# A softmax with its rows cut into ten tiles of thirteen and twelve rows instead of eleven of twelve and eight

## The chip, the cores and the metric

The kernel runs on one core of a Trainium2 chip. The metric is device time in microseconds, the median of several runs; lower is better. Besides, one execution of the kernel was recorded by the hardware profiler. Its times count from the first instruction of the program ("span").

A core has several engines that run their own instruction streams beside each other. Here three compute: VectorE (DVE) takes maxima and divides, ScalarE (ACT) takes exponentials, GpSimd (POOL) does next to nothing but issue transfers. SyncE (SP) only issues transfers. Transfers between the large memory (HBM) and the on-chip memory run on 16 DMA engines, which all queues share. Each stream is executed in order, and an instruction that waits holds up all behind it on its engine.

## The reference

The input is x of 32 x 512 rows with 1024 float32 each, and a temperature of 0.5. Each row is scaled and goes through a softmax:

```python
scaled = x / temperature
shifted = scaled - np.max(scaled, axis=-1, keepdims=True)
exp_x = np.exp(shifted)
return (exp_x / np.sum(exp_x, axis=-1, keepdims=True)).astype(np.float32)
```

So 67.1 MB are read and 67.1 MB written, and every element is looked at three times on the chip: for the maximum, for the exponential (with the sum of the row taken along), and for the division.

## The kernel before, in words

The 16384 rows are 128 for each of 128 partitions. They are cut into eleven tiles. A tile of k rows holds k rows of 4 KB in each partition, and takes a block of 128 x k neighbouring rows, so that each partition's share is one contiguous piece of k x 4 KB in HBM. The list `PASSES` (line 10) names the tiles, and how each is split into groups for the computation: `[4, 4, 4]`, nine times `[6, 6]`, and `[4, 4]`. Each number is the rows of a group; a tile's rows are their sum: 12 for ten tiles, 8 for the last. In this text tiles count from 0, so that tile 10 is the last.

A tile is loaded into one of four buffers by one transfer (line 60, issued by SP), computed in place, and stored by one transfer (line 108). With 12 rows of 4 KB, four buffers hold 48 rows, 192 KB in each partition. The pool of buffers goes round: tile i uses the buffer of tile i - 4, so its load waits until the store of tile i - 4 has landed.

For each group the kernel does three things:

- `maximum`: one instruction on DVE for the maxima of all rows of the group (line 69), and a small one that turns them into the bias -max/temperature (line 72).
- `exponential`: one instruction on ACT for each row (line 78), exp(x/temperature + bias), which also gives the row's sum.
- `divide`: the reciprocals of the sums (line 90, DVE), then the division, as one DVE instruction over the whole group (line 93) for the tiles in `WHOLE`, or one for each row (line 96) for the others.

`store` does something only with the last group of a tile: it issues the tile's transfer and then the load that waits for it. The stores of the tiles below `BY_POOL` are issued by POOL, the others by ACT. Ahead of the first store POOL reads one element of tile 2, and so waits until tile 2 has been loaded.

The order is written out by hand, and no scheduler changes it. In the loop over the groups the maximum and the exponential of group g stand ahead of the division and the store of group g - 1. So DVE has always a maximum to do while ACT takes exponentials. For the first group of a tile from `ALONE` on the order is turned round: the group before is divided and its tile stored first. In ACT's stream a store that ACT issues stands at the same place: behind the exponentials of the next tile's first group, or, from `ALONE` on, ahead of them.

Of the kernel before, what the change touches and what calls it, by code (L numbers as in the profile page):

```python
# [1 line left out]

# [4 lines left out]

PASSES = [[4, 4, 4]] + [[6, 6]] * 9 + [[4, 4]]  # L10
BUFS = 4

WHOLE = (2, 3, 4, 6, 8)


BY_POOL = 6

ALONE = 9


@with_exitstack
def kernel(
    ctx: ExitStack,
    tc: tile.TileContext,
    x: bass.AP,
    temperature: bass.AP,
    out: bass.AP,
):
    nc = tc.nc
    f32 = mybir.dt.float32  # L30
    scale = 1.0 / float(temperature)
    extreme = mybir.AluOpType.max if scale > 0 else mybir.AluOpType.min

    P = 128
    xf = x.flatten_outer_dims()
    of = out.flatten_outer_dims()
    n, d = xf.shape
    rows = [sum(ks) for ks in PASSES]
    assert sum(rows) * P == n

    data = ctx.enter_context(tc.tile_pool(name="data", bufs=BUFS))
    stats = ctx.enter_context(tc.tile_pool(name="stats", bufs=4))


    groups = []
    for i, ks in enumerate(PASSES):
        for j, k in enumerate(ks):
            groups.append((i, sum(ks[:j]), k))

    def dram(t, i):  # L50
        block = t[P * sum(rows[:i]) : P * sum(rows[: i + 1]), :]
        return block.rearrange("(p k) d -> p k d", p=P, k=rows[i])

    tiles, small = [], []

    def load():
        i = len(tiles)
        if i < len(PASSES):
            xt = data.tile([P, rows[i], d], f32, name="xt")
            nc.sync.dma_start(out=xt, in_=dram(xf, i))  # L60
            tiles.append(xt)

    def maximum(g):
        i, a, k = groups[g]
        top, bias, sums, recip = (
            stats.tile([P, k], f32, name=name) for name in ("top", "bias", "sums", "recip")
        )
        small.append((bias, sums, recip))
        nc.vector.tensor_reduce(  # L69
            out=top, in_=tiles[i][:, a : a + k, :], axis=mybir.AxisListType.X, op=extreme  # L70
        )
        nc.vector.tensor_scalar_mul(bias, in0=top, scalar1=-scale)  # L72

    def exponential(g):
        i, a, k = groups[g]
        bias, sums, _ = small[g]
        for b in range(k):
            nc.scalar.activation(  # L78
                tiles[i][:, a + b, :],
                tiles[i][:, a + b, :],  # L80
                mybir.ActivationFunctionType.Exp,
                bias=bias[:, b : b + 1],
                scale=scale,
                accum_out=sums[:, b : b + 1],
            )

    def divide(g):
        i, a, k = groups[g]
        _, sums, recip = small[g]
        nc.vector.reciprocal(recip, sums)  # L90
        if i in WHOLE:
            xt = tiles[i][:, a : a + k, :]
            nc.vector.tensor_mul(xt, xt, recip.unsqueeze(2).to_broadcast([P, k, d]))  # L93
            return
        for b in range(k):
            nc.vector.tensor_scalar_mul(  # L96
                tiles[i][:, a + b, :], in0=tiles[i][:, a + b, :], scalar1=recip[:, b : b + 1]
            )

    def store(g):  # L100
        i, a, k = groups[g]
        if a + k == rows[i]:
            if i == 0:


                nc.gpsimd.tensor_copy(stats.tile([P, 1], f32, name="seen"), tiles[2][:, 0, 0:1])  # L106
            queue = nc.gpsimd if i < BY_POOL else nc.scalar
            queue.dma_start(out=dram(of, i), in_=tiles[i])  # L108
            load()

    with tc.manual_schedule():
        for _ in range(BUFS):
            load()
        for g in range(len(groups) + 1):

            alone = g < len(groups) and groups[g][0] >= ALONE and groups[g][1] == 0
            if g > 0 and alone:
                divide(g - 1)  # L120
                store(g - 1)
            if g < len(groups):
                maximum(g)
                exponential(g)
            if g > 0 and not alone:
                divide(g - 1)
                store(g - 1)


# [1 line left out]
_INS = ['x', 'temperature']  # L131
_OUTS = [((32, 512, 1024), 'float32')]

_NUMBERS = {'temperature': 0.5}


# [26 lines left out]
```

## Time and profile before

| what | value |
|---|---|
| median of 3 runs | 317.25 us (317.19 to 320.41) |
| span of the profiled execution | 315.8 us |
| DVE busy | 256.9 us (81%) |
| ACT busy | 148.3 us (47%) |
| POOL busy | 3.7 us (1%) |
| mean rate of the DMA engines | 425 GB/s |
| maximum of 6 rows / of 4 rows (line 69) | 6547 ns / 4413 ns |
| exponential of one row (line 78) | 1135 ns |
| division of 6 rows at once (line 93) | 6558 ns |
| division of one row (line 96) | 749 ns |
| load of 12 rows, issue to landing, median | 36.4 us |
| store of 12 rows, issue to landing, median | 35.9 us by POOL, 31.9 us by ACT |

How to read it: the durations are those of single instructions as the profiler recorded them; neighbours on one engine overlap a little (row-wise divisions start 0.68 us apart, row-wise exponentials 1.13 us). "Issue to landing" holds all the time in which a transfer shares the DMA engines with others. A maximum of 6 rows costs 1.07 us for each row and some 0.1 us besides.

Between the span and the time of a run lies what is ahead of the program's first and behind its last recorded instruction: the median of the runs is 1.5 us above the span of the profiled execution.

### The profile page before, as it was taken

What the parts mean: (1) busy time and instruction counts of PE and PEld (TensorE: products, weight loads), DVE (VectorE), ACT (ScalarE), POOL (GpSimd) and SP (SyncE); (2) the same over time, 40 slices, a digit from 0 to 9 for tenths busy, and PEclk for the clock granted to TensorE, in tenths of its full rate; (3) what the DMA queues carried; (4) which work ended last, traced back from release to release, by engine and by line L of the source; (5) the groups of instructions that cost most, each with busy time, mean ns of one, the idle gap of its engine ahead of it and who ended that gap; (6) DMA issues with size and microseconds to landing.
All of it is one profiled execution on the core that took longest, in us unless ns stands there. A gap on an engine that the chain in (4) does not pass through costs nothing.

```text
span 315.8 us, 525 instructions
## 1 busy us (share of the span) xinstructions
DVE 256.9 (81%) x147; ACT 148.3 (47%) x257; POOL 3.7 (1%) x11
## 2 busy tenths in 40 slices
DVE  0069999999999899979976994999199999969710
ACT  0029636775461807344471744074416802953700
POOL 0000001000000000000000000000000000000000
DMA  8999999999999999999999999999999999999996
GB/s 305 473 417 423 461 411 399 399 468 430 400 479 417 417 461 411 430 467 405 442 448 399 455 442 405 467 424 417 461 417 430 455 401 463 411 452 411 455 411 270
DMA packets 3171, 134.24 MB, mean 425 GB/s; under 512 B 352, under 2 KB 352, under 8 KB 352
## 3 DMA queue, kind: packets, MB, share of 16 engines
q1 hardware_dynamic: 1584, 67.11, 49.7%
q0 software_dynamic: 864, 37.75, 27.6%
q10 hardware_dynamic: 720, 29.36, 21.5%
q14 instruction: 3, 0.02, 0.0%
HBM read 67.11 MB, written 67.11 MB: 425 GB/s over the span
## 4 chain that ended last, share of the span: by engine, by line
DMA 47%; DVE 28%; ACT 11%; issue 9%; DVEq 0%; SPq 0%; POOLq 0%
DMA xt<-in_x_dram 25%; DMA out_dram<-xt 22%; DVE top L69 16%; ACT xt L78 11%; DVE xt L96 8%; DVE xt L93 2%; DVE bias L72 0%; DVE recip L90 0%; DVEq L158 0%; SPq L60 0%; POOLq L108 0%
## 5 line engine op out<-in xcount | busy, mean ns | idle before, releaser
L78 ACT ACTIVATE xt<-xt,bias 128x1024 f32<-128x1024 f32 x128 | 145.2, 1135 | 131.7 <-DVE recip L90 70.6
L69 DVE TENSOR_REDUCE top<-xt 128x6 f32<-128x6144 f32 (+1 forms) x23 | 139.9, 6083 | 37.8 <-DMA xt<-in_x_dram 37.8
L93 DVE TENSOR_TENSOR xt<-xt,recip 128x6144 f32<-128x6144 f32 x10 | 65.6, 6558 | 0.4
L96 DVE TENSOR_SCALAR xt<-xt,recip 128x1024 f32<-128x1024 f32 x68 | 46.2, 749 | 0.5
L78 ACT ACTIVATION_READ_ACCUMULATOR xt<-xt,bias 128x1 f32 x128 | 23.9, 187 | 0.0
L78 ACT ACT_TABLE_LOAD x1 | 1.3, 1283 | 18.3 <-DMA xt<-in_x_dram 18.3
L90 DVE RECIPROCAL recip<-sums 128x6 f32<-128x6 f32 (+1 forms) x23 | 4.2, 182 | 5.0 <-ACT xt L78 5.0
L108 POOL DMA_DIRECT2D out_dram<-xt x6 | 3.3, 554 | 129.6 <-ACT xt L78 82.7
L72 DVE TENSOR_SCALAR bias<-top 128x6 f32<-128x6 f32 (+1 forms) x23 | 3.9, 171 | 0.8
L106 POOL COPY seen<-xt 128x1 f32<-128x1 f32 x1 | 0.2, 185 | 46.9 <-DMA xt<-in_x_dram 46.9
L144 POOL MEMSET const-uint8-127<- 128x1 uint8 x1 | 0.1, 103 | 0.0
L144 POOL MEMSET const-bfloat16-1.0<- 128x1 bf16 x1 | 0.1, 102 | 0.0
L144 POOL MEMSET const-float32-0.0<- 128x1 f32 x1 | 0.1, 99 | 0.2 <-issue 0.2
L144 POOL MEMSET const-float32-1.0<- 128x1 f32 x1 | 0.1, 98 | 0.0
## 6 DMA issues: line engine op xcount, KB each, us to landing
xt<-in_x_dram SPq DMA_DIRECT2D x10, 6144.0 KB, 36.4
out_dram<-xt POOLq DMA_DIRECT2D x6, 6144.0 KB, 35.9
out_dram<-xt ACTq DMA_DIRECT2D x4, 6144.0 KB, 31.9
xt<-in_x_dram SPq DMA_DIRECT2D x1, 4096.0 KB, 34.9
out_dram<-xt ACTq DMA_DIRECT2D x1, 4096.0 KB, 13.5
```

The costliest lines, as they stand in the source:

```text
L69: nc.vector.tensor_reduce(out=top, in_=tiles[i][:, a : a + k, :], axis=mybir.AxisListType.X, op=extreme)
L72: nc.vector.tensor_scalar_mul(bias, in0=top, scalar1=-scale)
L78: nc.scalar.activation(tiles[i][:, a + b, :], tiles[i][:, a + b, :], mybir.ActivationFunctionType.Exp, bias=bias[:, b : b + 1], scale=scal ...
L90: nc.vector.reciprocal(recip, sums)
L93: nc.vector.tensor_mul(xt, xt, recip.unsqueeze(2).to_broadcast([P, k, d]))
L96: nc.vector.tensor_scalar_mul(tiles[i][:, a + b, :], in0=tiles[i][:, a + b, :], scalar1=recip[:, b : b + 1])
L106: nc.gpsimd.tensor_copy(stats.tile([P, 1], f32, name="seen"), tiles[2][:, 0, 0:1])
L108: queue.dma_start(out=dram(of, i), in_=tiles[i])
L144: nc = _bacc.Bacc("TRN2", target_bir_lowering=False, num_devices=1)
```

## The change

The same rows are cut into ten tiles: eight of 13 rows and two of 12 rows (tiles 3 and 7). The list of groups becomes `[5, 4, 4]` for the first and the last tile, `[6, 6]` for tiles 3 and 7, and `[7, 6]` for the others. Tiles 0, 1, 2, 4, 5, 6, 8 and 9 go round in a pool of three buffers of 13 rows; tiles 3 and 7 have a pool with a single buffer of 12 rows. So the four buffers hold 51 rows, 204 KB in each partition, and tile i still uses the buffer of tile i - 4.

POOL issues the stores of tiles 0 to 3 and ACT those of tiles 4 to 9; before, POOL issued those of 0 to 5 and ACT those of 6 to 10. `ALONE` is 8 instead of 9: before, the turned order held for the last two of eleven tiles, now it holds for the last two of ten. Tile 8 leaves `WHOLE`.

```diff
-PASSES = [[4, 4, 4]] + [[6, 6]] * 9 + [[4, 4]]
+PASSES = [[5, 4, 4], [7, 6], [7, 6], [6, 6], [7, 6], [7, 6], [7, 6], [6, 6], [7, 6], [5, 4, 4]]
 BUFS = 4
 
-WHOLE = (2, 3, 4, 6, 8)
+WHOLE = (2, 3, 4, 6)
 
-BY_POOL = 6
+BY_POOL = 4
 
-ALONE = 9
+ALONE = 8
...
-    data = ctx.enter_context(tc.tile_pool(name="data", bufs=BUFS))
+    data = ctx.enter_context(tc.tile_pool(name="data", bufs=BUFS - 1))
+    short = ctx.enter_context(tc.tile_pool(name="short", bufs=1))
...
-            xt = data.tile([P, rows[i], d], f32, name="xt")
+            if i % BUFS == BUFS - 1:
+                xt = short.tile([P, rows[i], d], f32, name="xt")
+            else:
+                xt = data.tile([P, rows[i], d], f32, name="xt")
             nc.sync.dma_start(out=xt, in_=dram(xf, i))
```

## The prediction

> **What bounds the kernel now.** I read the page's engine busy times, slices and DMA queues first, then the DMA queues' own waits, then the timeline of the end, and for single transfers the trace's records of DMA packets (start and duration of each).
>
> From the page:
>
> ```profile
> span 315.8 us, 525 instructions
> ...
> DVE 256.9 (81%) x147; ACT 148.3 (47%) x257; POOL 3.7 (1%) x11
> ...
> DMA  8999999999999999999999999999999999999996
> ...
> q1 hardware_dynamic: 1584, 67.11, 49.7%
> q0 software_dynamic: 864, 37.75, 27.6%
> q10 hardware_dynamic: 720, 29.36, 21.5%
> ```
>
> The reader is to see that the three queues (loads; Pool's stores; ACT's stores) add to 98.8% of 16 DMA engines' span, 312.0 us of 315.8, while the busiest compute engine, DVE, has 59 us of slack. Only the first and the last slice are below 9. The windows view says the same by stretches: the DMA share is 0.99 to 1.01 from 3 to 305 us and 0.72 in the last 10.8 us.
>
> ```profile
> SPq L60 <- DMA out_dram<-xt: 241.2, 7, 74.3
> ```
>
> In the waits of SP's queue, every load after the first four waits for a store: a buffer is free when the store four tiles back has landed. Loads and stores then share the engines.
>
> The end of the run, from the timeline of DVE:
>
> ```profile
> 280.54 4.07 DVE L96 TENSOR_SCALAR xt<-xt,recip 128x1024 f32<-128x1024 f32 x6
> 284.52 4.41 DVE L69 TENSOR_REDUCE top<-xt 128x4 f32<-128x4096 f32 x1
> ...
> 289.04 4.41 DVE L69 TENSOR_REDUCE top<-xt 128x4 f32<-128x4096 f32 x1
> ...
> 293.84 0.18 DVE L90 RECIPROCAL recip<-sums 128x4 f32<-128x4 f32 x1 [0.18 <-ACT xt L78]
> 294.05 2.74 DVE L96 TENSOR_SCALAR xt<-xt,recip 128x1024 f32<-128x1024 f32 x4
> 298.36 0.18 DVE L90 RECIPROCAL recip<-sums 128x4 f32<-128x4 f32 x1 [1.57 <-ACT xt L78]
> 298.58 2.74 DVE L96 TENSOR_SCALAR xt<-xt,recip 128x1024 f32<-128x1024 f32 x4
> ```
>
> The last load (8 rows, issued at 246.68, 34.9 us to landing) lands at 281.6; its last packet ended at 279.5. Its store is issued at 301.35. That is 19.75 us of compute with no load left. What keeps the DMA engines busy meanwhile is the backlog of stores 8 and 9: by the packet records the last packet of store 9 ends at 304.8, and store 10 has its first at 303.1. So the **backlog** is 304.8 - 279.5 = 25.3 us; the **need** is 2.1 (last packet to landing) + 19.75 + about 1.0 (issue to first packet: 0.74 to 1.76 for the first load, on idle engines) = 22.9. Backlog exceeds need by 2.4 us, so nothing is lost. This margin decides the change.
>
> **The change, part by part.** The sum is made against the profiled execution, 315.8 us of span; the median of the runs, 317.25, is 1.5 above it, which I carry over.
>
> *Larger transfers.* A 48 KB packet takes 1.815 us and a 32 KB packet (last tile) 1.21 us: both 27.1 bytes/ns, so a packet costs by its bytes. 13 rows make 52 KB packets, estimated at 1.966. The bytes stay the same, and so do the 312 us: cost 0. No 52 KB packet is in this trace; the nearest rows, 32 and 48 KB, agree within 0.3%, which would be 1 us of the total either way. A gain is bounded too: some 2 us of packet time is above these rates (the first packets, 2.9 us instead of 1.8, and about twenty around the first store). If all of it and all idle engine time in the middle went, it would be 2 to 3 us.
>
> *Twenty transfers instead of 22.* The row: the first packets of loads 1, 2 and 3 come 14.5 us apart, which is 8 packets of 1.815 on each engine, so nothing stands between two transfers. I take 0. The Trainium skill says otherwise at first sight: in "DMA: Bandwidth & Descriptors", section "Anatomy of one DMA", each DMA has a fixed part of about 2 us, mostly the receipt of its last byte; two DMAs fewer would then be an estimate of 4 us saved, and 316.3 in place of my 320.3. The trace has such a delay, 2.1 us from last packet to landing, but other packets run during it.
>
> *The order on DVE, ACT and in the ring.* A load still waits for the store four tiles back: 51 rows are four tiles, not five. DVE does as many rows. The DVE work of a tile grows with its transfer time (about 29.0 us against a load and store of 31.5 us for a 13-row tile in WHOLE, 27.1 against 29.0 before). Costs in the middle: 0, hidden under the DMA.
>
> *Stores 4 and 5 go from POOL to ACT.* On ACT a store stands behind the exponentials of the next tile's first group. Seven of them take 7 x 1.134 = 7.9 us, where DVE needs 4.3 for reciprocal and 6-row division: store 5 is issued some 3.6 us later than DVE alone would allow; behind tile 4 it is about 1. What waits behind it is load 9, which needs store 5's buffer. In the loop load lands, maximum, exponential, store, load four tiles on, the trace of before has 2.5 + 14.0 + 7.2 + 26.9 + 2.3 + 7.2 + 26.9 = 87.0 us, three periods of 29.0. Both 7.2 (issue to first packet, under packets of the other queue) stretch: the first store had 4.4. After the change the fixed parts are 2.5 + 15.7 + 29.1 + 2.3 + 29.1 = 78.7 of 94.4, leaving 7.85 for each, so the loop still closes. Price 0; without that slack 3.6 us, kept in the range.
>
> *The front.* Store 1 must be there when store 0 ends. Store 0's last packet was at 76.8; four rows more in the first five transfers (64 for 60, 1.21 us each) give 81.6. Store 1 was issued at 69.5. DVE's chain to it gets longer by 1.2 (landing), 3 rows of maximum (3.2), 2 rows of division (1.4) and 1.2 more of wait for the five first exponentials: 76.5. It has 5.1 us to its first packet; POOL's first took 4.4. Price 0, but thin.
>
> *The end.* The last tile has 13 rows instead of 8, in groups of 5, 4, 4. From its landing, with DVE idle (tile 8 is divided before): maximum of 5 rows and bias 5.7; five exponentials 5.7, to 11.5; reciprocal and division of 5 rows 3.6, to 15.1; only then the last maximum of 4, 4.6, to 19.75; four exponentials 4.55, to 24.4; reciprocal and division 3.0, to 27.4. Need: 2.1 + 27.4 + 1.0 = **30.5** us.
>
> The backlog: the 25.3 us of before are 14 packets of 1.815 on each engine. The last load again comes when the store four tiles back has landed, its 8 packets again alternate with 8 store packets, and again three stores stand ahead of the last. So I keep 14 packets: 8 x 1.966 (tile 8) + 6 x 1.815 (tile 7) = 26.6 us. One packet more, which the different phase of the two queues may well leave, is 28.4. **The gap** in DMA work is then 30.5 - 26.6 = 3.9 or 30.5 - 28.4 = 2.1. I take the middle, 3.0, since no row favours either. As the last store (15.7 us) follows the gap and all else is the same work, the gap is added whole: 315.8 + 3.0 = 318.8 of span, and 317.25 + 3.0 = **320.3**. One packet fewer (24.8) gives a gap of 5.7.
>
> **The rivals.**
>
> *No gap.* If store packets pile up by two or three more (store queue behind by 4 us, as ACT's late stores could make it), backlog covers need, and the DMA sum alone stands: 316.3 to 318.0. For it: before has a margin, and stores 4 and 5 start later. Against: the engines interleave packet by packet, and a late store also delays the load behind it.
>
> *A second gap, slower.* POOL's later stores took 6.6 to 7.3 us from issue to first packet. If store 1 takes 7.3, there is nothing to move for 7.3 - 5.1 = 2.2 us at about 82: load 3 is done, load 4 waits for store 0. With the gap at the end 322.5. It decides from 5.1 us on. Against: those long delays were under the other queue's packets, and load 3 is done at about 73.
>
> *Faster.* The 2 us of slow packets vanish and there is no gap: 315. Under 314.1 (1% less) would need less than the bytes' own time at the packet rates.
>
> *The change doesn't do what it says.* If the separate pool broke the ring (tile 3 or 7 waiting for another buffer), a load would wait a whole tile more; the order of the instructions shows the same ring of four, so I give it next to nothing.
>
> **How the numbers follow.** The gap at the end alone, 319.3 to 321.2 with 320.3 as the likeliest: 0.57. No gap: 0.24. Second gap or a backlog of 13 packets, 322 to 323: 0.14. Faster than 316: 0.05. The range of 8 in 10 leaves out the fastest and the upper part of the slowest: 316.3 to 322.4. About 1% (3.2 us) is what a measurement of this kernel can tell from no change; the runs themselves go from 317.19 to 320.41. The line of 320.4 cuts my likeliest case nearly in the middle: of its 0.57 I put 0.27 below and 0.30 above. Slower by over 1%: 0.30 + 0.14 = 0.44. Within 1%: 0.27 + 0.24 + 0.02 = 0.53. Faster by over 1%: 0.03.
>
> **What would show it.** In the slices, DMA at 9 throughout and a dip in the two slices near 300 us. Last load landing at 274 to 277 us, last store issued 27.4 us later; the store before it ending 2 to 4 us before the last store's first packet. In the chain, more DVE and ACT between last load and last store. The queues together again about 312 us. Wrong if DMA time itself rises or falls (52 KB packets off 1.966), if the last store's packets join the one before without a pause, or if slices near 82 us show a dip.

## The result: slower by 2.6%

The changed kernel takes 325.97 us (median of 6 runs, 325.22 to 326.54) against 317.22 for the kernel before: a ratio of 1.0263, with a 95% interval of 1.0233 to 1.0293. That is 8.75 us more. The forecast was 3.0 us more, within 316.3 to 322.4. The direction and the place were right, the size was not.

The page of the changed kernel, the lines that answer to those shown of before:

```profile
span 324.2 us, 520 instructions
...
DVE 252.9 (78%) x151; ACT 148.2 (46%) x257; POOL 2.8 (1%) x9
...
DMA  8999999899999999999999999999999999997297
...
q1 hardware_dynamic: 1440, 67.11, 48.6%
q10 hardware_dynamic: 864, 40.37, 28.8%
q0 software_dynamic: 576, 26.74, 19.1%
```

The shares of the three queues add to 96.5% of 324.2, which is 312.9 us; before it was 312.0. So the transfers themselves cost nearly the same, and the span grew by time in which the DMA engines stand still. The slices show where: a single 2, the third from the end, between a 7 and a 9. By the packet records the mean idle time of an engine between its first and the run's last packet is 8.6 us, before 1.0.

The windows view of the same run (length, busy time of DVE, ACT and POOL with their instructions, clock, DMA share, GB/s):

```profile
75.00:164.00 89.00, 84.82 (x26) 46.90 (x83) 1.59 (x3) 1.00 1.00 435
164.00:178.00 14.00, 11.68 (x11) 8.54 (x16) 0.00 (x0) 1.00 1.00 432
178.00:297.00 119.00, 95.17 (x63) 53.84 (x94) 0.00 (x0) 1.00 1.00 433
297.00:308.00 11.00, 7.15 (x12) 4.64 (x8) 0.00 (x0) 1.00 0.22 92
```

Up to 297 us the engines are full all the time (0.99 from 3 to 75 us, by the same view); then they are busy for 22% of 11 us. Loads wait for stores as before (us in total, times, longest), and no DMA engine stands idle meanwhile:

```profile
SPq L65 <- DMA out_dram<-xt: 226.3, 6, 79.5
```

The end, from the timeline of DVE:

```profile
278.71 5.49 DVE L74 TENSOR_REDUCE top<-xt 128x5 f32<-128x5120 f32 x1 [4.94 <-DMA xt<-in_x_dram]
...
284.31 4.41 DVE L74 TENSOR_REDUCE top<-xt 128x4 f32<-128x4096 f32 x1
...
290.28 0.19 DVE L95 RECIPROCAL recip<-sums 128x5 f32<-128x5 f32 x1 [1.36 <-ACT xt L83]
290.51 3.40 DVE L101 TENSOR_SCALAR xt<-xt,recip 128x1024 f32<-128x1024 f32 x5
293.83 4.41 DVE L74 TENSOR_REDUCE top<-xt 128x4 f32<-128x4096 f32 x1
...
298.56 2.74 DVE L101 TENSOR_SCALAR xt<-xt,recip 128x1024 f32<-128x1024 f32 x4
303.21 0.18 DVE L95 RECIPROCAL recip<-sums 128x4 f32<-128x4 f32 x1 [1.91 <-ACT xt L83]
```

and the issue of the last store, from the timeline of ACT:

```profile
306.20 0.34 ACTq L113 DMA_DIRECT2D out_dram<-xt  x1
```

The last load's data is complete at 276.52 on the last of the 16 engines and lands at 278.69. DVE has stood idle for 4.94 us waiting for it and begins at once; the last store is issued at 306.20, and its first packet comes at 307.04. That is the need of the prediction, 307.04 - 276.52 = 30.5 us, to the tenth. But the store before it had its last packet at 301.29: a backlog of 24.8 and a pause of 5.75 us. On most engines the pause is longer still, since 15 of the 16 had finished that store by 299.3 (landings), and one at 301.6.

That last point is new. Each transfer raises its semaphore 16 times, once for each DMA engine, and the trace has the times. In the kernel before, the last engine is 1.2 us behind the median engine (the ninth of the 16 to be done) at the last load; in the changed kernel 5.2 us (273.5 and 278.7). A load counts as landed only when the slowest engine is done. Below, "lag" is this difference.

### The profile page after: what moved, and what is told of

It is laid out like the page before. It is cut to its first block, busy times and chain, and to the rows that moved or that the text cites. A ratio compares the mean times of both kernels' runs of the same rounds, so it can differ in the third digit from the quotient of the medians.

```text
span 324.2 us, 520 instructions
## 1 busy us (share of the span) xinstructions
DVE 252.9 (78%) x151; ACT 148.2 (46%) x257; POOL 2.8 (1%) x9
## 4 chain that ended last, share of the span: by engine, by line
DMA 62%; DVE 25%; ACT 6%; issue 0%; DVEq 0%; SPq 0%; ACTq 0%
DMA xt<-in_x_dram 40%; DMA out_dram<-xt 23%; DVE top L74 17%; DVE xt L101 7%; ACT xt L83 6%; DVE bias L77 0%; DVE recip L95 0%; DVEq L163 0%; SPq L65 0%; ACTq L83 0%
## 5 line engine op out<-in xcount | busy, mean ns | idle before, releaser
L74 DVE TENSOR_REDUCE top<-xt 128x6 f32<-128x6144 f32 (+3 forms) x22 | 139.8, 6354 | 41.1 <-DMA xt<-in_x_dram 41.1
L98 DVE TENSOR_TENSOR xt<-xt,recip 128x6144 f32<-128x6144 f32 (+1 forms) x8 | 55.7, 6959 | 0.4
L101 DVE TENSOR_SCALAR xt<-xt,recip 128x1024 f32<-128x1024 f32 x77 | 52.3, 749 | 0.5
L95 DVE RECIPROCAL recip<-sums 128x6 f32<-128x6 f32 (+3 forms) x22 | 4.1, 186 | 10.6 <-ACT xt L83 10.6
L77 DVE TENSOR_SCALAR bias<-top 128x6 f32<-128x6 f32 (+3 forms) x22 | 3.8, 171 | 0.8
L113 POOL DMA_DIRECT2D out_dram<-xt x4 | 2.3, 564 | 80.8 <-issue 28.9
```

The costliest lines, as they stand in the source:

```text
L74: nc.vector.tensor_reduce(out=top, in_=tiles[i][:, a : a + k, :], axis=mybir.AxisListType.X, op=extreme)
L101: nc.vector.tensor_scalar_mul(tiles[i][:, a + b, :], in0=tiles[i][:, a + b, :], scalar1=recip[:, b : b + 1])
```

## The experiments

The theories: **A**, the whole loss is the pause ahead of the last store (need less backlog); **B**, the 52 KB packets or the middle of the run; **C**, from the first store of ACT on, two store queues and the load queue share the engines for a while, which sets the loads back and puts an engine out of step. C came from the packet records: in the changed kernel ACT's store 4 has its first packet at 168.1 while POOL's store 3 has its last at 173.1. In the kernel before, POOL's last store ended at 217.22 and ACT's first began at 217.33.

The measured numbers, for reference (those of e5, e8 and e10 stand in the text). "Data" is when the last load's last packet ended, "pause" the time from the last packet of the store before the last to the first packet of the last store, "idle" the mean idle time of an engine.

| kernel | time, us | data | lag | backlog | need | pause | idle |
|---|---|---|---|---|---|---|---|
| before | 317.2 | 279.5 | 1.2 | 25.4 | 23.7 | none | 1.0 |
| changed | 326.0 | 276.5 | 5.2 | 24.8 | 30.5 | 5.75 | 8.6 |
| e1 changed, last tile raw | 319.3 | 276.3 | 5.1 | | | none | 2.7 |
| e3 changed, 6 stores by POOL | 323.5 | 274.4 | 1.4 | 24.8 | 30.5 | 5.7 | 7.1 |
| e4 changed, none by POOL | 320.2 | 270.7 | 1.5 | 28.4 | 30.5 | 2.1 | 3.4 |
| e9 changed, all by POOL | 320.7 | 270.1 | 0.9 | 28.4 | 31.0 | 2.6 | 3.5 |
| e6 as e4, maxima first | 317.9 | 270.5 | 1.5 | 28.4 | 27.1 | none | 1.0 |
| e11 changed, in turn (trace of the 348.0) | 333.3 to 348.0 | 296.5 | 21.7 | 11.6 | 32.5 | 20.8 | 30.1 |
| e2 before, 4 by POOL | 318.3 | 279.9 | 3.2 | 24.7 | 23.3 | none | 1.3 |
| e7 before, last tile 12 rows | 321.3 | 277.9 | 4.6 | 23.6 | 27.9 | 4.3 | 6.7 |
| e7b as e7, none by POOL | 322.6 | 276.5 | 2.9 | 25.4 | 27.9 | 2.5 | 4.3 |

**Is it all the pause? (e1)** e1 leaves out the exponentials and the divisions of the last tile.

```diff
     def exponential(g):
         i, a, k = groups[g]
+        if i == len(PASSES) - 1:
+            return
...
     def divide(g):
         i, a, k = groups[g]
+        if i == len(PASSES) - 1:
+            return
```

> The changed kernel, but tile 9 (the last) is stored without its exponentials and division; only its maxima are still taken, and its store waits for its load alone. So the 27.5 us of compute between the last landing and the last store are gone, and all transfers are the same. Theory A (all of the loss is the pause ahead of the last store, 7.7 us of idle engine time): the pause goes, and the time falls from 326.0 to 317.5 to 319.5. Rival B (the 52 KB packets, or waits in the middle, cost the time): it stays above 322.

Measured: 319.3 us, ratio to before 1.0052 (1.0031 to 1.0072). The pause is gone and 6.7 of the 8.75 us with it. Lag and lateness of the last load are as in the changed kernel (5.1; data at 276.3), but from 64 us on no slice except the last is below 9: while the queues are full they leave no engine idle. The 2 us that stay are mostly engines that finish apart: at the very end the last one is 3.3 us behind the median. Theory A holds for 6.7 us, and B falls for nearly all of the loss.

```profile
DMA  8999999799999999999999999999999999999993
```

**Does the meeting of the store queues matter? (e2, e3, e4, e9, e11)** In e2 the kernel before gets only the new split of the stores:

```diff
-BY_POOL = 6
+BY_POOL = 4
```

> The kernel before with one edit: POOL issues four stores, ACT seven. Theory C (where the first store of ACT runs beside the last store of POOL, three queues share the engines and one DMA engine falls out of step with the others): the last of the 16 engines lands loads 3 us or more after the median one from load 7 on (1.2 us in the kernel before), and the time rises by 1 to 4 us, since only 2.4 us of store backlog were to spare. Rival D (the engines fall out of step because 13-row and 12-row packets alternate): lag stays at 1.2 us, time 317.2.

Measured: 318.25, ratio 1.0028 (1.0002 to 1.0054). POOL's store 3 now overlaps ACT's store 4 (156.4 to 160.5 us), and the lag rises from 0.8 at load 5 to 2.5 at load 6 and 3.2 at the last load, with 12-row tiles up to that load. That is theory C, with lags a little under the 3 us expected at first and a price at the lower edge, since the short last tile leaves no pause. Rival D is not needed.

e3 and e4 move the split in the changed kernel instead.

```diff
-BY_POOL = 4
+BY_POOL = 6
```

> The changed kernel with POOL issuing six stores, as before the change. Theory C: POOL's store 5 and ACT's store 6 now meet, so the lag of the one engine is smaller up to load 8 and the time 322 to 325. Rival E (the stores of tiles 4 and 5 come earlier by the 1 and 3.6 us which ACT's exponentials cost, the store queue runs ahead, less backlog is left at the end): 327 to 331, with the last load landing no earlier than 278.7.

Measured: 323.5, ratio 1.018 (1.0141 to 1.0219). The queues meet later (store 6 from 227.8, store 5 until 233.4). The engines stay in step, lag 1.4, but load 8, which runs in that time, is complete at 243.4 instead of 239.4 without a meeting (e4), and the last load at 274.4 instead of 270.7. Rival E (an earlier store 5 as the harm) falls: store 5 was issued at 192.4, in e4 by ACT at 192.2. That a meeting puts an engine out of step, as C had it, does not hold here; that it sets the loads back does.

```diff
-BY_POOL = 4
+BY_POOL = 0
```

> The changed kernel with all stores issued by ACT, so two queues in all and no handover between store queues. Theory C: the last of the 16 engines lands loads at most 1.5 us after the median one (5.2 us at the last load in the changed kernel), the last load lands some 4 us earlier, and the time is 321 to 323. Rival D (mixed packet sizes put the engines out of step): lag of 3 us or more stays, 324 to 327.

Measured: 320.23, ratio 1.0081 (1.006 to 1.0103), under the range that C gave. Lag 1.5, backlog 28.4, need 30.5, pause 2.1. So 5.7 of the 8.75 us belong to the two store queues. Store 4 was issued by ACT at nearly the same time in both, as the line of the changed kernel and that of e4 show; its first packet came at 168.1 in the changed kernel and at 171.95 in e4, where store 3 stood ahead of it in the same queue until 169.94.

```profile
164.30 0.38 ACTq L113 DMA_DIRECT2D out_dram<-xt  x1
164.32 0.34 ACTq L113 DMA_DIRECT2D out_dram<-xt  x1
```

The DMA slices of e4 have a dip to 5 where the changed kernel had 2, and from 297 to 308 us its engines are busy for 73%, not 22%:

```profile
DMA  8999999799999999999999999999999999999597
297.00:308.00 11.00, 2.92 (x5) 0.30 (x2) 0.00 (x0) 1.00 0.73 315
```

The same with the queue of the other engine:

```diff
-BY_POOL = 4
+BY_POOL = 10
```

> The changed kernel with all stores issued by POOL. Theory C (the meeting of two store queues beside the loads costs, not POOL's queue itself): as with all stores by ACT, 320 to 321, lag of the last engine at most 1.6 us, last load's data complete at about 270.7. Rival F (a store that POOL issues is slower or puts an engine out of step): 322 to 326.

Measured: 320.73, ratio 1.0118 (1.0101 to 1.0134). It isn't POOL's queue that costs: rival F falls, and one store queue of either kind gives the same 320 to 321.

Then the suspected cost many times over:

```diff
-            queue = nc.gpsimd if i < BY_POOL else nc.scalar
+            queue = nc.gpsimd if i % 2 == 0 else nc.scalar
```

> The changed kernel with stores issued by POOL and ACT in turn, so that store queues can meet nine times instead of once. Theory C as it stands (each meeting gives the loads a third of the engines instead of half, for a few packets, and sets them back against the stores): the loads fall back further each time, 327 to 335. Variant C2 (a load set back makes the next store later by as much, so the next meeting is avoided and the loss stays that of one meeting): 322 to 327. If meetings cost nothing: 320 to 321, as with one store queue.

Measured: 333.29 to 347.97 in four runs, 334.99 and 344.43 the other two; two fit C as it stands (ratio of these two 1.0526, 1.0488 to 1.0564), two lie above it. C2 falls. The only trace is that of the slowest run (347.97), so what it shows holds for that execution alone, not for the two near 334 us. There the last load is in on the median engine at 278.9 and on the last one at 300.6. DVE waits for that one engine, as its next maximum shows:

```profile
300.64 5.49 DVE L74 TENSOR_REDUCE top<-xt 128x5 f32<-128x5120 f32 x1 [25.57 <-DMA xt<-in_x_dram]
```

The slices of its page show the engines nearly empty from 294 to 329 us, first while that engine catches up and then during the last tile's compute, with nothing left to store:

```profile
DMA  9999999999999999999999999999999999300096
```

**Is the pause the price of the last tile's compute? (e6, e7, e7b, e5, e10)** e6 takes e4, with one store queue, and changes only the order in the last tile: all three maxima, then the divisions.

```diff
-BY_POOL = 4
+BY_POOL = 0
...
             if g > 0 and not alone:
-                divide(g - 1)
-                store(g - 1)
+                if g == len(groups):
+                    for h in range(g - len(PASSES[-1]), g):
+                        divide(h)
+                        store(h)
+                elif groups[g - 1][0] < len(PASSES) - 1:
+                    divide(g - 1)
+                    store(g - 1)
```

> The changed kernel with all stores by ACT (320.2 us, one pause of 2.1 us), and in the last tile all three maxima ahead of the divisions. By the durations of the rows the compute after the last landing falls from 27.5 to 24.3 us. Theory (pause = need less backlog, added whole): need 2.1 + 24.3 + 0.9 = 27.3 is under the backlog of 28.4, the pause goes, 317.5 to 318.5. Rival (the pause is not what costs): 320 stays.

Measured: 317.89, ratio 1.0022 (1.0011 to 1.0033). Last landing to last store took 24.1 us instead of 27.5; need 27.1 is under the backlog of 28.4, the pause is gone, and with it 2.3 us. So all of the change is in but the split of the stores and the order within the last tile, and the time is within 0.3% of before.

```profile
DMA  8999999899999999999999999999999999999995
```

e7 makes the last tile large without any 52 KB packet: the 8-row tile of the kernel before moves to the front.

```diff
-PASSES = [[4, 4, 4]] + [[6, 6]] * 9 + [[4, 4]]
+PASSES = [[4, 4]] + [[6, 6]] * 10
```

> The kernel before with its 8-row tile at the front and 12 rows in the last tile: no 52 KB packets, no change of queues except that the six POOL stores start with a smaller tile. Need by the rows: 2.1 + 24.8 + 0.9 = 27.8 us; with 14 packets of backlog 25.4, a pause of 2.4 and 319.6; with 15 packets 27.2, a pause of 0.6 and 317.8. Theory (size of the last tile alone makes a pause): 317.8 to 320. Rival (13-row packets make it): 317.2 or less and no pause.

Measured: 321.28, ratio 1.014 (1.0098 to 1.0183); runs from 320.42 to 323.5, the profiled one the slowest. Over the range of A, and again with a meeting: POOL's store 5 until 209.5, ACT's store 6 from 204.4, a lag of 0.9 before and 3.4 to 4.6 after. So it was run once more with one store queue:

```diff
-BY_POOL = 6
+BY_POOL = 0
```

> The kernel before with its 8-row tile at the front, 12 rows in the last tile, and all stores by ACT, so that no two store queues meet: the size of the last tile alone. Need by the rows 2.1 + 24.8 + 0.9 = 27.8 us; backlog of 15 packets of 1.815 (as many as with all stores by ACT in the changed kernel) 27.2, of 14 packets 25.4. Theory A: a pause of 0.6 to 2.4 us and 317.8 to 319.6. Rival B (52 KB packets make the loss): no pause, 317.2 or less.

Measured: 322.58, ratio 1.0164 (1.0134 to 1.0194). Need 27.9 (27.8 worked out), backlog 25.4 (the 14 packets), pause 2.5: the account of the end holds and rival B falls, since 48 KB packets make the pause as well. The total missed its range by 3 us, for things that the account leaves out: packets that take longer than 1.815 us around the first stores (1.3 us of engine time more than before), and a lag of 2.9 us, here from load 5 on with only two queues. A meeting of store queues is thus not the only thing that puts engines out of step. Nor did the time fall when the second store queue went: 322.58 after 321.28 us in e7, with intervals that overlap. In this pair no price of a meeting is seen.

e5 and e10 cut the last 13 rows into tiles of 8 and 5 rows, with four stores by POOL and with none.

```diff
-PASSES = [[5, 4, 4], [7, 6], [7, 6], [6, 6], [7, 6], [7, 6], [7, 6], [6, 6], [7, 6], [5, 4, 4]]
+PASSES = [[5, 4, 4], [7, 6], [7, 6], [6, 6], [7, 6], [7, 6], [7, 6], [6, 6], [7, 6], [4, 4], [5]]
```

> The changed kernel, the last tile of 13 rows cut into two tiles of 8 rows (groups 4, 4) and 5 rows (one group); eleven tiles, POOL still issues four stores. Theory A with C: the pause ahead of the last store goes, since three stores stand ahead of a tile that needs some 15 us of compute, while the engines stay out of step from the meeting of the two store queues on: 317.5 to 319.5. Rival B: the loss is spread over the middle, 322 or more.

Measured: 320.0, ratio 1.0101 (1.0046 to 1.0157), runs from 318.53 to 323.04. Most of the loss is gone; it comes out half a microsecond over the range. The lag is there as expected, 5.0 at the last load, and part of a pause stays (1.4 us of idle time near 308).

> The changed kernel with both causes undone: all stores by ACT, and the last 13 rows as two tiles of 8 and 5. Theories A and C together: engines in step, no pause at the end, 316.5 to 318. If something else in the 13-row tiles costs, 319 or more. A time under the kernel before would need the slow packets near the first store to go, which neither theory expects.

Measured: 318.61, ratio 1.0042 (1.0028 to 1.0055), 0.6 over the range: no pause, idle 1.6, packets 0.5 us longer in sum, lag 2.1.

Last, the kernel before with all stores by ACT:

> The kernel before with all stores by ACT. In the kernel before POOL's last store had ended when ACT's first began, so theory C expects nothing to gain from undoing the handover: 316.6 to 317.4. Rival F (POOL's queue costs by itself): 315.5 or less.

Measured: 317.66, ratio 1.0005 (0.9989 to 1.002). No gain and no loss that can be told: in the kernel before the handover from POOL to ACT cost nothing. None of the versions beats the kernel before; at 312 us of full engines and 1 us of idle time it has hardly anything to give.

## Why the prediction was wrong in size

- **What bounds the kernel**: right. DMA time is 312.0 us before and 312.9 us after, by the queues' shares.
- **Larger transfers, price 0**: right within the 1 us that it allowed. The median 52 KB packet took 1.966 us, as estimated; slower ones, near the first store and between 240 and 260 us, make 0.8 us more of engine time in sum than before.
- **Twenty transfers instead of 22, nothing saved**: right, no saving is seen: e6, with 20 transfers and no pause, takes 317.89 us. The fixed part for each DMA, quoted from the Trainium skill ("DMA: Bandwidth & Descriptors", "Anatomy of one DMA"), gave an estimate of 316.3; the prediction took it for all transfers, while that section states it for those issued by GpSimd. What the trace has of such a delay (2.2 us from the last load's last packet to landing, 0.35 us for the last store, which has the engines to itself) counts once, in the need at the end.
- **The front, price 0**: right. Store 0 ended at 82.1, store 1 was issued at 76.2 and had its first packet at 81.0, after 4.8 us; no slice dips there. (The 6.6 to 7.3 us that the prediction gives for POOL's later stores leave out store 5 of before, 10.2 us.)
- **The need, 30.5 us**: right, measured 30.5, with 27.5 of compute for 27.4.
- **The step that failed: "Stores 4 and 5 go from POOL to ACT", price 0.** I looked at what stands ahead of the store on ACT and in the loop, and not at the other queue. A store on POOL's queue waits behind POOL's store before it; here ACT's store 4 didn't, and had its first packet at 168.1 us, before the last one of POOL's store 3 ended at 173.1. The price is 325.97 - 320.23 = 5.7 us by e4, and 5.2 us by e9. The 3.6 us that I did name there weren't there either (below). The last load landed at 278.7 us, later than the 274 to 277 that were to show the forecast right.
- **The backlog**: I took the middle between 14 and 15 packets, 3.0 us of pause. With one store queue it is 15 packets, 28.4 us, pause 2.1, and 320.23 us, 0.1 from the forecast; part of that nearness is luck, since the pause is 0.9 us shorter than forecast and small terms that the sum left out make it up. With the meeting it is 24.8, the value that I gave for one packet fewer and put into a rival with 0.14; that rival's 322 to 323 us is still 3 us short.
- **"The gap is added whole"**: only with the engines in step (in e3 a pause of 5.7 us and a time 6.3 us above before). A lagging engine makes the last load late for all and the pause longer on the 15 others: 5.75 us of pause on the last engine came with 7.7 us more idle time in the mean than before, and 0.8 us longer packets make up the 8.46 us of span.

How the 5.7 us divide between loads set back and the engine out of step can be read from the traces in part. The last load lands 5.87 us later than in e4 (278.69 and 272.82), and the last store follows it by the same 27.5 us. Of that, 2.14 us are on the median engine, and 3.73 us are lag. e3 has the meeting, at another place, with all engines in step: its last load lands 3.7 us later than in e4, all of it on the median engine, and it is 3.3 us over e4; the changed kernel is 2.5 over e3. What each would cost without the other in the changed kernel isn't shown.

## What to carry to other kernels

Where the DMA engines are full, look at the end first: the compute between the last load's landing and the last store has to fit into the stores that are still queued, so the last tile should be small or its order short. Try all stores on one queue, or a handover from one issuer to another only when the first one's transfers are done: a second store queue takes turns from the loads. That was worth 5.2 to 5.7 us in the changed kernel, some 1 us between the kernel before and e2, and nothing that can be told between e7 and e7b. And a transfer is as late as its slowest engine, so the spread of its 16 semaphore increments is worth a look where waits don't add up.

## What the runs showed of the hardware that was not expected

**A third queue and the loads.** With one store queue beside the loads (e4), load 8 was complete at 239.4 us; with two for some 5 us (e3) at 243.4, two packets of 1.97 us later, and the loads behind it did not make that up (274.4 and 270.7 for the last). By the packet records the loads had 30% of the engines' time from 227.8 to 233.4 us in e3 and each store queue 35%; in e4 the loads had 65% in the same stretch, since its one store queue has no packet between two stores from 231.55 to 233.56. In the changed kernel few packets really overlap: when ACT's first one came at 168.1 us, 2 of the 128 of POOL's store 3 had yet to start (16 in e3). What the second queue does there is above all that store 4 begins 3.85 us earlier than in e4; from 168.1 to 173.1 us the loads get 49% of the engines and not 77%.

**Engines out of step.** One of the 16 engines, in e1 and e7 two, can fall behind with loads while none is idle: by 5.2 us in the changed kernel, by 21.7 in the traced run of e11. Why these engines and not the others, and why e3 has a meeting without it, stays open. It differs between executions too: e1 and the changed kernel are the same program up to the last tile, and the lag at load 4 was 1.1 and 1.6 us, at store 1 1.0 and 2.6.

**A new queue's first packet.** In the kernel before, ACT's first store waited 6.1 us from issue to first packet, just until POOL's last store had ended; in the changed kernel, e2 and e3 it was 3.5 to 4.0 us, before POOL's had ended. That there was no meeting before hangs on this, and it isn't settled.

**ACT's stores don't wait for exponentials ahead of them.** From the timeline of the changed kernel, at store 5:

```profile
191.96 1.15 ACT L83 ACTIVATE xt<-xt,bias 128x1024 f32<-128x1024 f32 x1 [14.15 <-DVE bias L77]
...
192.05 4.07 DVE L101 TENSOR_SCALAR xt<-xt,recip 128x1024 f32<-128x1024 f32 x6
...
196.15 0.34 ACTq L113 DMA_DIRECT2D out_dram<-xt  x1
...
196.51 1.13 ACT L83 ACTIVATE xt<-xt,bias 128x1024 f32<-128x1024 f32 x1
...
198.77 1.13 ACT L83 ACTIVATE xt<-xt,bias 128x1024 f32<-128x1024 f32 x1
```

Seven exponentials stand ahead of the store in ACT's program, and they run from 191.96 to 199.9. The store was issued at 196.15, right after DVE's division ended, and three of the seven began after it. So its place behind them in ACT's stream did not hold this store up, and the 3.6 us of delay in the prediction did not exist.
